# Moving a modulation slab from behind the linear half to behind the value products, in the prompt attention loop of a decoder step

## The chip, the cores and the metric

The kernel runs on one core of one Trainium2 chip. The metric is the device time of one execution in microseconds; a change is compared by the median of several runs. The engines are called as in the profile: PE is the matrix engine (TensorE), with PEld for its weight loads, DVE is VectorE, ACT is ScalarE, POOL is GpSimd, and SP is the engine whose queue issues most DMAs.

## The reference, cut to what matters

One step of a decoder layer for a prompt of 512 tokens and 32 sample tokens. The two groups share all weights. The parts that meet in the stage under study are these:

```python
mod = jax.nn.silu(c) @ w['w_ada'] + w['b_ada']            # six modulation vectors
sh1, sc1, g1, sh2, sc2, g2 = jnp.split(mod[:, None, :], 6, axis=-1)
...
y_a = (bg * v) @ w['w_out_conv']                           # the convolution branch's projection
...
s_s = jnp.einsum('bqgrd,bgqnkd->bgrqnk', q, k_sel) - slopes * s_dist
p_s = jax.nn.softmax(jnp.where(tok_valid, s_s, NEG), axis=(-2, -1))
o_s = jnp.einsum('bgrqnk,bgqnkd->bqgrd', p_s, v_sel)
s_w = jnp.einsum('bqgrd,bkgd->bgrqk', q, kw) - sl * w_dist
p_w = jax.nn.softmax(jnp.where(w_valid, s_w, NEG), axis=-1)
o_w = jnp.einsum('bgrqk,bkgd->bqgrd', p_w, vw)
o = gates[..., 0:1] * o_c + gates[..., 1:2] * o_s + gates[..., 2:3] * o_w
...
x = x + g1 * ((ga * y_a + gb * y_b) @ w['w_out'])
```

There are 16 heads in 4 groups of 4. Of the modulation vectors the later ones (for the gates and the second norm) are needed only after the attention, so their products with `w_ada` can be computed at any time before that.

## The kernel before, in words

The kernel is one long straight program. It is written line by line, and the framework that compiles it puts the instructions of each engine into an order of its own planning: it goes by the order in the program, and where an instruction would have to wait it may place a later one first. The order on the chip is then fixed.

The prompt attention is a loop (lines 1511 to 1531) over the 4 head groups `g` and, in each, the query blocks `i` = 3, 2, 1, 0 of 128 queries. One pair is a unit; block `i` attends to 128(i+1) keys, so block 3 is the largest. A unit is a generator in two halves (`unit`, line 1417):

- Scores. For each of the 4 heads and the 2 branches (selected and window) PE multiplies queries and keys into an accumulator `sp` (lines 1431 to 1439), DVE adds the distance penalty and takes the extremum (line 1444), and ACT takes the exponential with its sum (line 1445). Then DVE makes the factors `fac` (lines 1449 and 1450) and scales the eight probability tiles `P` (line 1457). Tiles of odd and of even blocks have eight buffers each.
- Value products. PE transposes the compressed branch's probabilities (`ctp`, line 1462), which ACT copies (`pct`), then for every 128 keys and each branch four transpositions into one accumulator (`ptp`, line 1472). Each such accumulator is copied to a tile `PT`, five times of six by ACT, the sixth time by DVE (`pev`, lines 1386 and 1388). Two products per 128 keys (`acc`, line 1466) and eight of the compressed branch (line 1482) gather the output; ACT and DVE move it to `oT` (lines 1484 and 1485).

Three further kinds of work are put between these in each iteration:

- A linear half (`oc_gen`, line 1366): 24 matmuls (lines 252 to 254) of the convolution branch's output projection, one half of the tokens for one block of 128 columns. Its weights come as 1 MB slabs, four in all, and are split by ACT and DVE into a high and a low part (lines 247 and 248). SP loads a tile `ga` for each half, and DVE multiplies by it (line 1378).
- A modulation slab (`mod_slab`, line 426): 32 matmuls (line 432) of `w_ada`, 256 columns a slab, run in four column strips of the array (128\*32); ACT copies the sum (`m`, line 434), and the slab before is finished by a transposition (`modq`, line 443) and two small DVE additions. SP loads a slab of 1 MB into one of three buffers `raw`, which the linear slabs use too.
- `presum` (line 561): copies of weights for later stages, a DMA by SP and an adding DMA by POOL.

The order in an iteration before the change is: scores of the unit, a linear half, a modulation slab, `presum`, the value products of the unit before. The accumulators of the linear half, `modp`, `modq`, `ctp`, `ptp` and some scores share five banks; two more serve scores, one serves `acc`.

Of the kernel before, what the change touches and what calls it, by code (L numbers as in the profile page):

```python
# [156 lines left out]
def build(tc, a, o):  # L157
# [19 lines left out]
    def tp_ps(nm):  # L177
        return ps.tile([128, 512], F32, tag="g", bufs=5, name=nm)
# [9 lines left out]
    def nm(s):  # L188
        uid[0] += 1
        return f"{s}_{uid[0]}"  # L190
# [44 lines left out]
    def slab(*key):  # L235
        nk, ncol = len(SLABS[key][1]), SLABS[key][2].shape[-1]
        v = raw_tile("raw")[:, 0:nk * ncol]
        last_slab[0] = queue(lambda: sync.dma_start(v, a["wt"][SLAB_AT[key], :, 0:nk * ncol]))
        return v.rearrange("p (k f) -> p k f", k=nk)
# [186 lines left out]
    def mod_slab(s, v=None):  # L426
        v = slab("ada", s) if v is None else v
        p = tp_ps(nm("modp"))
        for k in range(KC):
            for hh in range(2):  # L430
                j = (k % 2) * 2 + hh
                pe.matmul(p[32 * j:32 * j + 32, 0:128], lhsT=cT[:, k, :], rhs=v[:, k, hh * 128:(hh + 1) * 128], start=(k < 2), stop=(k >= 6))  # L432
        m4 = wpool.tile([128, 128], F32, tag="m4", bufs=2, name=nm("m4"))
        act.activation(m4, p[:, 0:128], AF.Copy)
        if modp:
            modp.pop()()
        modp.append(lambda: mod_fin(s, m4))
# [3 lines left out]
    def mod_fin(s, m4):  # L441
        q = tp_ps(nm("modq"))
        pe.transpose(q[:, 0:128], m4, ident)
        qv = q[:, 0:128].rearrange("p (a h n) -> p a h n", a=2, h=2)
        dst = modT[:, 2 * s:2 * s + 2, :]
        bb = badaT[:, 2 * s:2 * s + 2].rearrange("p (h x) -> p h x", x=1).broadcast_to([128, 2, 9])
        dve.tensor_add(dst, qv[:, 0, :, 0:9], bb)
        dve.tensor_add(dst, qv[:, 1, :, 0:9], dst)
# [112 lines left out]
    def presum(n=1):  # L561

        done = copied[:]
        del copied[:]
        for _ in range(min(n, len(pre_keys))):
            key = pre_keys.pop(0)
            w_ = len(SLABS[key][1]) // 4 * 128
            t = pre[key] = dr.tile([128, 1024], F32, name=nm("pre"))
            src = a["wt"][SLAB_AT[key], :, 0:4 * w_].rearrange("p (n f) -> p n f", n=4)
            dst = t[:, 0:2 * w_].rearrange("p (n f) -> p n f", n=2)  # L570
            with tc.issue_after(last_slab[0].ins):
                sync.dma_start(dst, src[:, 0:1].broadcast_to([128, 2, w_]))
            copied.append((dst, src[:, 1:4:2]))
        for dst, src in done:
            pool.dma_start(dst, src, accum_op=ALU.add)  # L575
# [762 lines left out]
    def k_stack(g):  # L1338
        gp, me = g // 2, slice((g % 2) * 64, (g % 2) * 64 + 64)
        kh, kl = ks_[g % 2]  # L1340
        for n, t in enumerate((kh, kl)):
            for b in range(2):
                sync.dma_start(t[b * 64:b * 64 + 64].rearrange("p b x -> p (b x)").bitcast(F32), k_dr[gp][n][me])
        return kh, kl

    def q_stack(g):
        gp, me = g // 2, slice((g % 2) * 64, (g % 2) * 64 + 64)
        t = qs_[g % 2]
        for n in range(2):
            sync.dma_start(t[n * 64:n * 64 + 64].rearrange("p r x -> p (r x)").bitcast(F32), q_dr[gp][n][me])  # L1350
        return t
# [38 lines left out]
    def cmp_probs(g, qs):  # L1390
        p = tp_ps(nm("cpt"))
        for r in range(4):
            pe.matmul(p[32 * r:32 * r + 32, :], lhsT=kcd[:, g, :], rhs=qs[:, r, :].bitcast(F32), start=True, stop=True)
        ct = at.tile([128, 512], F32, tag="PT", bufs=4, name=nm("cpT"))
        act.activation(ct, p, AF.Copy)
        cps = s_ps(nm("cps"))
        for i in range(4):
            pe.transpose(cps[:, i * 128:(i + 1) * 128], ct[:, i * 128:(i + 1) * 128], ident)
        pc = pcs[g % 2] if g else pc0
        v3 = pc.rearrange("p i r c -> p (i r) c")  # L1400
        m, sm = (at.tile([128, 16], F32, tag=n, bufs=2, name=nm(n)) for n in ("cm", "csm"))
        bc = lambda z: z.rearrange("p (n x) -> p n x", x=1).broadcast_to([128, 16, 32])
        cd = t_cd.rearrange("p i (x c) -> p i x c", x=1).broadcast_to([128, 4, 4, 32])
        sl = slr[:, g, :].rearrange("p (y r x) -> p y r x", y=1, x=1).broadcast_to([128, 4, 4, 32])
        dve.tensor_add(pc, cps.rearrange("p (i r c) -> p i r c", i=4, r=4), cd)
        dve.tensor_mul(pc, pc, sl)
        dve.tensor_reduce(m, v3, axis=AX.X, op=ALU.max)
        dve.tensor_sub(v3, v3, bc(m))
        act.activation(pc, pc, AF.Exp)
        dve.tensor_reduce(sm, v3, axis=AX.X, op=ALU.add)  # L1410
        dve.reciprocal(sm, sm)
        dve.tensor_mul(sm.rearrange("p (i r) -> p i r", i=4), sm.rearrange("p (i r) -> p i r", i=4), gtok[:, :, g * 12:(g + 1) * 12].rearrange("p i (r b) -> p i r b", b=3)[:, :, :, 0])
        dve.tensor_scalar_mul(sm[:, 0:4], sm[:, 0:4], rowv)
        pool.tensor_tensor(v3, v3, bc(sm), op=ALU.mult)
        return pc
# [95 lines left out]
    prev = None  # L1511
    nslab = 8
    ocf = oc_gen()
    for g in range(4):
        qs, ks = qst, kst
        pc = cmp_probs(g, qs) if g else first_pc
        for i in (3, 2, 1, 0):
            u = unit(g, i, ks, qs, pc) if g or i < 3 else first_unit
            if g or i < 3:
                next(u)  # L1520
            next(ocf, None)
            mod_slab(nslab, mods_ahead.pop(0) if mods_ahead else None)
            nslab += 1
            presum(g > 0 or i < 2)
            if prev is not None:
                next(prev, None)
            prev = u
            if g < 3 and i == 3:
                qst = q_stack(g + 1)
            if g < 3 and i == 2:  # L1530
                kst = k_stack(g + 1)
# [554 lines left out]
```

## Time and profile before

| what | us |
|---|---|
| median of 3 runs | 1193.41 (1191.88 to 1194.09) |
| the profiled execution | 1191.61 |
| its span in the profile | 1189.8 |
| the 512 slab matmuls of the loop (line 432), busy | 19.1 |
| the value products `acc` (line 1466) in the loop, busy | 44.4 |
| the transpositions `ptp` (line 1472) of tiles `P` in the loop, busy | 36.8 |

The times of the timeline are counted from the start of the span. A row of the timeline has the start, the duration, the engine, the line, the operation, the tiles written and read, the shape, the number of like instructions merged into the row, and in brackets the idle time ahead of it with what ended it. Matmuls are pipelined: the distance from one start to the next tells what one costs, and the duration, which overlaps the next one's, does not.

### The profile page before, as it was taken

The page shows a single profiled execution, that of the slowest core. Times are in us where ns is not written, and L with a number is a line of the kernel's source. Part 1 is how long each engine was busy: PE and PEld are TensorE (multiplying, and loading weights), DVE is VectorE, ACT ScalarE, POOL GpSimd, SP SyncE. Part 2 cuts the span into 40 slices and gives each one's busy share as a digit, 9 for nine tenths or more (in the row PEclk, how much of TensorE's full clock was granted, in tenths as well). Part 3 has the DMA queues.
Part 4 walks back from the last instruction along what each step waited for, and adds up shares of the span by engine and source line. Part 5 has one row for each costly group of instructions (what it writes and reads, how often), then busy time and mean ns, then how long its engine had stood idle before and what let it go on. Part 6 is the DMA issues. An engine that isn't in the chain of part 4 may idle for free.

```text
span 1189.8 us, 25820 instructions
## 1 busy us (share of the span) xinstructions
PE 1177.5 (99%) x10114; PEld 1094.1 (92%) x10114; DVE 854.2 (72%) x1927; ACT 641.0 (54%) x1302; POOL 103.8 (9%) x154
## 2 busy tenths in 40 slices
PE   9999999999999999999999999999999999999997
PEld 7999999999999888887777879999999999999996
DVE  2539986888775576686767866758848888887776
ACT  1416544665455333386766765527646566666541
POOL 1000151000000111020101100000010001001000
PEclk9999999999999999999999999999999999999999
DMA  9963465878656998979887779444356358349412
GB/s 334 368 230 125 143 221 161 256 239 245 212 193 192 357 371 315 304 216 263 223 221 224 209 201 315 172 163 169 91 150 200 129 141 242 119 126 219 173 54 75
DMA packets 86283, 248.81 MB, mean 209 GB/s; under 512 B 9480, under 2 KB 19592, under 8 KB 74522
## 3 DMA queue, kind: packets, MB, share of 16 engines
q1 hardware_dynamic: 73330, 222.77, 53.6%
q0 software_dynamic: 12112, 23.09, 12.1%
q8 instruction: 79, 1.29, 0.4%
q10 hardware_dynamic: 720, 1.31, 0.3%
q14 instruction: 42, 0.34, 0.1%
HBM read 216.33 MB, written 65.28 MB: 237 GB/s over the span
## 4 chain that ended last, share of the span: by engine, by line
PE 92%; DVE 4%; DMA 2%; ACT 1%; issue 1%; POOL 0%; DVEq 0%; ACTq 0%; POOLq 0%
PE wA L254 8%; PE wA L252 8%; PE wA L253 8%; PE phi L676 7%; PE lin L252 7%; PE lin L253 7%; PE lin L254 7%; PE wC L253 4%; PE wC L254 4%; PE wC L252 4%; PE acc L1466 3%; PE ptp L1472 3%; PE modp L432 2%; PE wB L252 2%; PE wB L254 2%; PE wB L253 2%
## 5 line engine op out<-in xcount | busy, mean ns | idle before, releaser
L412 ACT ACTIVATE Wh<-raw 128x1024 fp32r<-128x1024 f32 (+2 forms) x82 | 62.1, 757 | 49.7 <-PE wA L253 34.9
L413 DVE TENSOR_TENSOR Wl<-raw,Wh 128x1024 fp32r<-128x1024 f32 (+2 forms) x82 | 70.1, 855 | 21.9 <-ACT Wh L412 21.4
L301 ACT ACTIVATE work<-wA 128x272 f32<-128x272 f32 x102 | 40.1, 393 | 73.6 <-PE wA L254 73.4
L1445 ACT ACTIVATE P<-P,nms 128x384 f32<-128x384 f32 (+3 forms) x120 | 65.0, 545 | 20.1 <-DVE nms L1444 19.2
L1444 DVE CUSTOM_DVE_ANT_0 P<-sp,ta 128x384 f32<-128x384 f32 (+3 forms) x120 | 52.2, 469 | 30.2 <-PE sp L1432 22.7
L252 PE MATMUL lin<-h_h,wh 128*128 128x288 f32 (+1 forms) x240 | 71.5, 298 | 0.0
L413 DVE TENSOR_TENSOR wl<-ws,wh 128x1024 fp32r<-128x1024 f32 (+1 forms) x50 | 59.1, 1182 | 16.3 <-ACT wh L412 15.1
L412 ACT ACTIVATE wh<-ws 128x1024 fp32r<-128x1024 f32 (+1 forms) x50 | 51.3, 1026 | 33.8 <-PE wC L253 23.2
L253 PE MATMUL lin<-h_l,wh 128*128 128x288 f32 (+1 forms) x240 | 69.3, 289 | 0.0
L413 DVE TENSOR_TENSOR wl<-raw,wh 128x1024 fp32r<-128x1024 f32 (+2 forms) x56 | 65.9, 1177 | 4.5 <-ACT wh L412 4.2
L254 PE MATMUL lin<-h_h,wl 128*128 128x288 f32 (+1 forms) x240 | 69.1, 288 | 0.0
L247 ACT ACTIVATE wh<-raw 128x1024 fp32r<-128x1024 f32 (+1 forms) x43 | 41.9, 976 | 41.7 <-PE lin L253 25.8
L248 DVE TENSOR_TENSOR wl<-raw,wh 128x1024 fp32r<-128x1024 f32 (+1 forms) x43 | 48.3, 1123 | 21.0 <-ACT wh L247 20.8
L412 ACT ACTIVATE wh<-raw 128x1024 fp32r<-128x1024 f32 (+2 forms) x56 | 56.1, 1001 | 12.6 <-PE wB L253 5.1
L676 PE MATMUL phi<-gt,wphi 128*128 128x128 f32 x512 | 61.3, 277 | 0.0
L676 PEld LDWEIGHTS phi<-gt,wphi 128*128 128x128 f32 x512 | 59.1, 192 | 1.9 <-issue 1.1
L575 POOL DMA_DIRECT2D pre<-in_wt x28 | 27.4, 977 | 349.1 <-DMA pre<-in_wt 335.1
L252 PE MATMUL wA<-S_hi,Wh 128*128 128x272 f32 x184 | 53.3, 290 | 0.6 <-ACT work L301 0.6
L254 PE MATMUL wA<-S_hi,Wl 128*128 128x272 f32 x184 | 53.1, 289 | 0.0
L253 PE MATMUL wA<-S_lo,Wh 128*128 128x272 f32 x184 | 53.0, 289 | 0.0
L252 PEld LDWEIGHTS lin<-h_h,wh 128*128 128x128 f32 x240 | 45.6, 190 | 7.5 <-issue 6.2
L253 PEld LDWEIGHTS lin<-h_l,wh 128*128 128x128 f32 x240 | 45.2, 188 | 0.1
(586 smaller groups left out, 4366.0 us busy)
## 6 DMA issues: line engine op xcount, KB each, us to landing
raw<-in_wt SPq DMA_DIRECT2D x68, 1024.0 KB, 6.7
raw<-in_wt SPq DMA_DIRECT2D x24, 768.0 KB, 5.3
sraw<-in_cache_sel SPq DMA_DIRECT2D x64, 256.0 KB, 5.4
gt<-in_cache_cmp SPq DMA_DIRECT2D x60, 256.0 KB, 5.7
pre<-in_wt SPq DMA_DIRECT2D x20, 512.0 KB, 8.8
pre<-in_wt POOLq DMA_DIRECT2D x20, 512.0 KB, 7.0
wraw<-in_cache_winT SPq DMA_DIRECT2D x8, 1024.0 KB, 7.8
raw<-pre SPq DMA_DIRECT2D x20, 256.0 KB, 6.6
```

The lines of the kernel that those rows point to most:

```text
L247: act.activation(oh, view, AF.Copy)
L248: dve.tensor_sub(ol, view, oh.bitcast(F32))
L252: pe.matmul(p, lhsT=wh[:, k, :], rhs=xh, start=start, stop=False, **kw)
L253: pe.matmul(p, lhsT=wh[:, k, :], rhs=xl, start=False, stop=False, **kw)
L254: pe.matmul(p, lhsT=wl[:, k, :], rhs=xh, start=False, stop=stop, **kw)
L301: o_.snap_ops.append(act.activation(t, p, AF.Copy))
L412: act.activation(hi, src, AF.Copy)
L413: return dve.tensor_sub(lo, src, hi.bitcast(F32))
L676: pe.matmul(po[:, c0:c0 + 128], lhsT=w[:, ch], rhs=x[:, :, ch * 16:ch * 16 + 16], start=(n_ == 0 and ch == 0), stop=(n_ == 2 and ch == 7))
L1444: p_ops.append(dve.tensor_tensor_reduce(out=t[:, 0:n], in0=sps[br], in1=t_dist[:, 512 - n:512], scale=-hs, scalar=3e38, op0=ALU.add, op1=A ...
L1445: e_ops.append(act.activation(t[:, 0:n], t[:, 0:n], AF.Exp, scale=-1.0, bias=nms[:, c:c + 1], accum_out=sums[:, c:c + 1]))
L1466: pe.matmul(acc[br * 64:br * 64 + 64, :], lhsT=vtok[br][:, j, g * 64:(g + 1) * 64], rhs=pts_[br], start=(j == 0), stop=False)
```

## The change

The call of `mod_slab` and `presum` moves behind the step of the previous unit's value products. In the new order an iteration has: scores of the unit, a linear half, the value products of the unit before, a modulation slab, `presum`. In the first iteration there is no unit before, and nothing changes there.

```diff
             if g or i < 3:
                 next(u)
             next(ocf, None)
+            if prev is not None:
+                next(prev, None)
+            prev = u
             mod_slab(nslab, mods_ahead.pop(0) if mods_ahead else None)
             nslab += 1
             presum(g > 0 or i < 2)
-            if prev is not None:
-                next(prev, None)
-            prev = u
             if g < 3 and i == 3:
                 qst = q_stack(g + 1)
             if g < 3 and i == 2:
                 kst = k_stack(g + 1)
```

## The prediction

> **What bounds the kernel now.** I read the page first, then the busy time of each engine in the attention stage, then the idle waits of TensorE there, and last the order of the instructions around a few modulation slabs.
>
> ```profile
> span 1189.8 us, 25820 instructions
> PE 1177.5 (99%) x10114; PEld 1094.1 (92%) x10114; DVE 854.2 (72%) x1927; ACT 641.0 (54%) x1302; POOL 103.8 (9%) x154
> ```
> ```profile
> 515.00:718.00 203.00, 202.42 (x1755) 153.18 (x1753) 145.16 (x513) 139.55 (x385) 22.23 (x25) 1.00 0.80 225
> ```
> ```profile
> PE acc L1466 <- ACT PT L1386: 0.3, 1, 0.3
> PE sp L1431 <- DVE nms L1444: 0.3, 1, 0.3
> ```
>
> The second fence is the stage that the change touches, all sixteen units of it: its length, then the busy time of TensorE, of its weight loads, of VectorE, ScalarE and GpSimd, then the granted clock (1.00). TensorE is busy for 202.42 of 203.00 us, and the third fence holds the only two waits that its matmul row shows, 0.3 us each. A busy row is not yet a full engine, so I looked at the distances between starts in one iteration (group 1, query block 1):
>
> ```profile
> 593.45 0.30 PE L253 MATMUL lin<-yin_lo,wh 128*128 128x288 f32 x1
> 593.58 0.29 PE L254 MATMUL lin<-yin_hi,wl 128*128 128x288 f32 x1
> 593.80 1.08 PE L432 MATMUL modp<-raw,cT 128*32 128x128 f32 x32
> 594.82 0.33 PE L443 MATMUL modq<-ident,m 128*128 128x128 f32 x1
> 594.98 0.27 PE L1462 MATMUL ctp<-ident,pc 128*128 128x128 f32 x1
> 595.09 1.91 PE L1472 MATMUL ptp<-ident,P 128*128 128x128 f32 x16
> 596.93 1.57 PE L1466 MATMUL acc<-PT,vtok 128*64 128x512 f32 x4
> ...
> 649.18 1.08 PE L1466 MATMUL acc<-PT,vtok 128*64 128x512 f32 x4
> ```
>
> Here the order of before is seen: linear half, slab (modp, with the transposition modq of the slab before), then the value products of the unit before (ctp, ptp, acc). Linear matmuls follow each other every 0.13 us and everything else is as tight, with one exception: the first four value products took 1.57 us where the same four took 1.08 us one group later. So TensorE sets the end of this stage, nothing can be gained by hiding work behind it, and the change can gain or lose only what alters TensorE's own intervals: changes of array layout, and waits of the value products for their copies.
>
> **What the change does, part by part.** It adds and removes no instruction. The slab's 32 matmuls and the modq transposition go from ahead of the previous unit's value products to behind them, in 15 of 16 iterations (the first has no previous unit). From the start of modp to the start of ctp the block is 594.98 - 593.80 = 1.18 us. The value products start that much earlier, the next unit's scores start when they did. Priced step by step:
>
> (a) *Layout.* From the last linear matmul to modp it is 593.80 - 593.58 = 0.22 us instead of 0.13: 0.09 us for going from the full array (128\*128) to four column strips (128\*32). After the change a linear matmul is followed by ctp, full width.
>
> ```profile
> 641.34 0.39 PE L1431 MATMUL sp<-kh,qs 128*128 128x512 f32 x1
> 641.57 0.40 PE L1432 MATMUL sp<-kl,qs 128*128 128x512 f32 x1
> ```
> ```profile
> 580.04 0.40 PE L1431 MATMUL sp<-kh,qs 128*128 128x512 f32 x1
> 580.27 1.47 PE L1472 MATMUL ptp<-ident,P 128*128 128x128 f32 x12
> ```
>
> No row shows that pair; the nearest is a score matmul before a transposition, both of full width, and it takes 0.23 us like two scores in a row (641.57 - 641.34), so no extra. At the other end modp follows the two-strip products, where a full-width score follows now: a change of layout either way. The gain lies between 0 and 0.09 us an iteration; I take 0.09, from the nearest row. In 12 iterations (the other three are priced whole in b): -1.1 us.
>
> (b) *The three iterations of block 2 in groups 1 to 3.* Here the previous unit is the large one (block 3), and ScalarE is late:
>
> ```profile
> 576.75 0.28 PE L254 MATMUL lin<-yin_hi,wl 128*128 128x256 f32 x1
> 576.96 0.41 PE L432 MATMUL modp<-raw,cT 128*32 128x128 f32 x2
> 577.30 0.45 PE L1438 MATMUL sp<-kh,qs 128*128 128x384 f32 x1
> ...
> 577.85 1.07 PE L432 MATMUL modp<-raw,cT 128*32 128x128 f32 x30
> 578.85 0.33 PE L443 MATMUL modq<-ident,m 128*128 128x128 f32 x1
> ...
> 581.67 0.65 PE L1466 MATMUL acc<-PT,vtok 128*64 128x512 f32 x2
> ```
> ```profile
> 578.78 0.60 ACT L1445 ACTIVATE P<-P,nms 128x384 f32<-128x384 f32 x1
> ...
> 579.67 0.27 ACT L1463 ACTIVATE pct<-ctp 128x128 f32<-128x128 f32 x1
> 580.00 0.60 ACT L1386 ACTIVATE PT<-ptp 128x512 f32<-128x512 f32 x1
> 580.97 1.09 ACT L1386 ACTIVATE PT<-ptp 128x512 f32<-128x512 f32 x2 [0.37 <-PE ptp L1472]
> ```
>
> ScalarE runs the new unit's exponentials until 579.4, and only then the copies (pct, PT) that the value products read. Before, slab and scores covered that, and the first product started at 581.67. After, the transpositions can begin at 576.9; sixteen take 1.84 us (595.09 to 596.93), the scores placed among them some 1.3 us (the pair at 577.30 takes 0.55; three single ones follow, estimated at 0.25 each), so TensorE is ready at 580.1. The copies are not: pct can move up to some 579.5, two PT follow at 0.54 us (1.09 for two) by about 580.85. So the products start 0.82 us earlier, not 1.18: a loss of 0.36 us, three times, +1.1 us. The bounds are 0 (copies planned ahead of the exponentials) and 1.18 each.
>
> (c) *Group 1, block 1, the late product above.* Its second copy is VectorE's:
>
> ```profile
> 594.50 2.19 DVE L1457 TENSOR_SCALAR P<-P,fac 128x256 f32<-128x256 f32 x8
> ...
> 596.69 0.69 DVE L1388 COPY PT<-ptp 128x512 f32<-128x512 f32 x1
> ```
>
> The copy stands behind the eight scalings of the new unit and ends at 597.4. The scalings hang on that unit's scores, which don't move. TensorE would be ready at 593.71 + 0.11 + 1.84 = 595.7 and still get the copy at 597.4, and the slab comes on top afterwards: +1.2 us, once. Lower bound 0, if the copy is planned ahead.
>
> (d) *The four iterations of block 0.* ScalarE has a 1 us weight split at the front:
>
> ```profile
> 553.00 1.04 ACT L247 ACTIVATE wh<-raw 128x1024 fp32r<-128x1024 f32 x1
> ...
> 554.76 1.58 ACT L1386 ACTIVATE PT<-ptp 128x512 f32<-128x512 f32 x3 [0.15 <-PE ptp L1472]
> ```
> ```profile
> 555.97 1.08 PE L1466 MATMUL acc<-PT,vtok 128*64 128x512 f32 x4
> ```
>
> After the change the split still ends at 554.04; pct (0.28) and two copies put the products at about 555.5, against 555.97 now. They would start 0.47 us earlier instead of 1.18, a loss of 0.7 us unless the slab, which is next in the program and needs none of these copies, fills the hole. Four copies fit into the five shared accumulators with room for the slab once ctp is read, so I take 0 and keep 4 x 0.7 = 2.9 us as the other end. Block 3 has small value products (two copies) and the same filler: 0.
>
> (e) *Queues.* The slab's load (1 MB) waits on SP for a buffer that an earlier slab frees, and now frees later by one unit's value products, about 8.5 us for the largest (eight tiles, each four transpositions at 0.115 us and two products at 0.25, and small ends).
>
> ```profile
> 579.31 0.38 SPq L238 DMA_DIRECT2D raw<-in_wt  x1
> ...
> 594.41 0.33 SPq L1374 DMA_DIRECT2D ga<-ga_dr  x1
> ```
> ```profile
> raw<-in_wt SPq DMA_DIRECT2D x68, 1024.0 KB, 6.7
> ```
>
> The load at 579.31 goes out 0.5 us after a slab's last matmul (578.85, where modq follows it). It would go to some 588, land at 595 after 6.7 us, and still be ahead of the ga load queued behind it, which waits for its own tile until 594.41. With three buffers a slab is loaded two iterations ahead of its matmuls, over 20 us by the iterations above (modp at 576.96, 593.80 and then 12 us later), so a landing 8.5 us later is still early. SP's order and GpSimd's additions don't change. Price 0; without that slack it would be up to 6.7 us a load.
>
> **Sum.** -1.1 + 1.1 + 1.2 + 0 + 0 = +1.2 us on the profiled execution's 1191.61, which is 1192.8. That execution lies 1.8 us under the median shown (1193.41), so for a median I say **1194.6**.
>
> [...] One PT copy takes ScalarE 0.53 us (1.58 for three), the four transpositions and two products behind it take TensorE about 0.96 (0.46, from 1.84 for sixteen, and half of the 1.0 that four products take), so the copies do not set the pace unless they start late. [...]
>
> **The rivals.**
>
> *Slower: copies stay behind the new unit's work.* Place: the four block-0 iterations (d). If the slab isn't planned into the hole behind the weight split, 2.9 us come on top: 1197.5 (+0.34%). It decides from the point where more than half of them go unfilled. For it: TensorE takes its matmuls in order (the wait of 0.3 us for nms had linear work right behind it), and the plan missed the late copy in c already. Against it: score pieces are placed in such holes elsewhere (577.30).
>
> *Faster: the plan moves the copies ahead.* Then b and c cost nothing, the layout gains 15 x 0.09 = 1.35, and what is lost now goes: 0.49 in c (1.57 less 1.08), the two waits of 0.3, and the slab cut in two by scores in b, which takes 1.89 us from 576.96 to 578.85 of which the scores are 0.55, so 0.3 over an uncut 1.02, three times. -1.35 - 1.1 - 0.9 = -3.4 us: 1190.0.
>
> *It doesn't do what it says.* The order on an engine is planned when the kernel is compiled, not written line by line (the scores inside the slab show it). If the slab is taken as the filler of the value products' first wait, it runs nearly where it did: 1193.4.
>
> *TensorE has room after all.* Its weight loads are busy 153.18 of 203.00 us, 75%, beside 99.7% for its matmuls. If that quarter were free, the slab could vanish from the path between products and scores: 15 x 1.18 = 17.7 us, 1175.7. [...] The starts 0.13 and 0.23 us apart without gaps speak against it here: long matmuls simply need few loads.
>
> **How the numbers follow.** A measurement of this kernel can tell about 0.2%, 2.4 us, from no change. Forecast with the third rival, both within that: 0.55. Slower by the first rival, or by several of b to d at their upper ends: 0.25. Faster by the second: 0.18, by the fourth: 0.02. So faster 0.20, same 0.55, slower 0.25. The range takes in the first two rivals and a little of the spread of the runs (1191.88 to 1194.09): 1189.5 to 1198.2.
>
> **What would show it.** Right: linear to ctp at 0.13 us; products at 580.85 or so in the block-2 iterations; a stretch of the same stage between 202 and 207 us; PE waits for PT growing from 0.3 to about 3 us. Wrong: copies standing ahead of exponentials and scalings (then faster), waits for PT in the block-0 iterations too (slower), or a difference that lies outside the stage.

## The result, and the profile after

The changed kernel takes **1203.87 us** (median of 6 runs, 1202.09 to 1207.71), the kernel before 1192.74 us in the runs beside it (6 runs, 1191.33 to 1194.09). The ratio is 1.0092, with a 95% interval of 1.008 to 1.0104: the change costs 11 us. The forecast was 1194.6, in a range of 1189.5 to 1198.2. Beside the runs further down, the kernel before had medians of 1192.74 to 1193.97; every ratio is to the kernel before in the same rounds, and a difference between medians of different rounds is good to about 1 us.

The head of the page after, then two views of the attention stage: its row with busy times (up to the point where the kernel before stood at 718.25, which is 728.58 here), and the waits of TensorE in it (total, times, longest; `nms` is the extremum that a scoring on VectorE writes):

```profile
span 1200.3 us, 25830 instructions
PE 1180.9 (98%) x10114; PEld 1095.2 (91%) x10114; DVE 856.4 (71%) x1927; ACT 639.0 (53%) x1302; POOL 103.8 (9%) x154
```
```profile
515.00:728.00 213.00, 206.81 (x1758) 155.11 (x1758) 147.74 (x514) 138.37 (x387) 22.25 (x25) 1.00 0.77 210
```
```profile
PE acc L1466 <- ACT PT L1386: 3.7, 4, 1.9
PE lin L252 <- DVE nms L1444: 1.8, 2, 1.1
PE ptp L1472 <- ACT pct L1463: 0.7, 1, 0.7
```

The span grew by 10.5 us, the stage by as much (728.58 less 718.25 is 10.3), and the rest of the kernel is unchanged. In the stage TensorE now stands idle for 6.2 us (213.00 less 206.81; 0.6 before), and its busy time grew by 4.4 although its matmuls are the same ones: a busy row that grows without new work is a row with stretched intervals.

To see where the time went I cut the stage at the last linear matmul of each iteration, so that every piece holds one linear half, one slab, one unit's value products and about one unit's scores. For instance, in group 1 the piece with the value products of block 3 took 593.58 - 576.75 = 16.83 us before (rows of the prediction), and after:

```profile
581.37 0.28 PE L254 MATMUL lin<-yin_hi,wl 128*128 128x256 f32 x1
...
597.63 0.30 PE L254 MATMUL lin<-yin_hi,wl 128*128 128x288 f32 x1
```

That is 16.26 us. (The end is the start of the last linear matmul in both.) Pieces are named by the block whose value products they hold. The piece of block 0 lies in the block-3 iteration, that of block 3 in the block-2 iteration, and so on. Blocks 0 and 3 follow each other, and scores slip between them, so they are added. Sums over the groups, in us (of blocks 1 and 0 the last group has no linear half of this loop behind it and is missing):

| kernel | blocks 0 and 3 | block 2 | block 1 |
|---|---|---|---|
| before | 91.86 | 47.14 | 43.10 |
| after | 96.31 (+4.45) | 51.32 (+4.18) | 44.49 (+1.39) |

Two places of about equal size, then, each with its own mechanism in the trace.

**Place one: a weight split that waits for its load, ahead of the copies.** Group 2, value products of block 2, ScalarE and TensorE after:

```profile
652.30 0.49 ACT L1445 ACTIVATE P<-P,nms 128x256 f32<-128x256 f32 x1
...
654.93 1.06 ACT L247 ACTIVATE wh<-raw 128x1024 fp32r<-128x1024 f32 x1 [2.04 <-DMA raw<-in_wt]
655.90 0.26 ACT L1463 ACTIVATE pct<-ctp 128x128 f32<-128x128 f32 x1
656.05 2.05 ACT L1386 ACTIVATE PT<-ptp 128x512 f32<-128x512 f32 x4
```
```profile
652.68 0.30 PE L254 MATMUL lin<-yin_hi,wl 128*128 128x288 f32 x1
652.82 0.27 PE L1462 MATMUL ctp<-ident,pc 128*128 128x128 f32 x1
652.92 1.91 PE L1472 MATMUL ptp<-ident,P 128*128 128x128 f32 x16
656.70 1.56 PE L1466 MATMUL acc<-PT,vtok 128*64 128x512 f32 x4 [1.86 <-ACT PT L1386]
...
677.58 0.30 PE L252 MATMUL lin<-yin_hi,wh 128*128 128x288 f32 x1
```

The split (wh, line 247) waits 2.04 us for its slab to land and then works 1.06 us. The copies pct and PT stand behind it, though the transpositions they read began at 652.8, and TensorE stands still for 1.86 us. The split is the first of a new slab. The linear half that ends at 652.68 and the one from 663.22 on still read weights of the slab before, split at 610.88; the half that reads the new ones starts at 677.58, over 22 us later: nobody was in a hurry for the split. It merely stood first in the queue: in these rows ScalarE begins none of the copies in the 2.04 us in which the split waits, and takes them behind it (655.90 and 656.05).

The load is late because the block-2 slab, whose buffer it takes, is now later. Its issue on SP (SPq is SP's queue), before (632.21) and after (647.67), and the same split before. Counted from the last linear matmul of the iteration (629.66 and 637.99), the load goes out after 2.55 us before and after 9.68 us now, 7.1 us later:

```profile
632.21 1.04 SPq L238 DMA_DIRECT2D raw<-in_wt  x1
```
```profile
647.67 0.33 SPq L238 DMA_DIRECT2D raw<-in_wt  x1
```
```profile
640.49 1.06 ACT L247 ACTIVATE wh<-raw 128x1024 fp32r<-128x1024 f32 x1 [0.53 <-DMA raw<-in_wt]
```

Already before, the split waited 0.53 us for this load, behind all copies of block 3's value products. The load had no slack at all at its first reader in this group, and that row stood in the trace when I predicted.

**Place two: the scores of block 2 start late.** The start of group 1's block-3 iteration, TensorE and then VectorE, before:

```profile
568.71 1.04 PE L1472 MATMUL ptp<-ident,P 128*128 128x128 f32 x8
569.50 0.71 PE L1438 MATMUL sp<-kh,qs 128*128 128x384 f32 x2
570.05 0.52 PE L1439 MATMUL sp<-kl,qs 128*128 128x384 f32 x2
...
571.22 1.30 PE L1466 MATMUL acc<-PT,vtok 128*64 128x512 f32 x4
```
```profile
570.43 0.56 DVE L1444 CUSTOM_DVE_ANT_0 P<-sp,ta 128x384 f32<-128x384 f32 x1 [0.64 <-PE sp L1439]
...
572.01 3.26 DVE L1457 TENSOR_SCALAR P<-P,fac 128x512 f32<-128x512 f32 x8
```

and after:

```profile
569.43 1.03 PE L1472 MATMUL ptp<-ident,P 128*128 128x128 f32 x8
570.22 0.42 PE L1438 MATMUL sp<-kh,qs 128*128 128x384 f32 x1
570.57 0.62 PE L432 MATMUL modp<-raw,cT 128*32 128x128 f32 x10
571.12 1.07 PE L1466 MATMUL acc<-PT,vtok 128*64 128x512 f32 x2
572.12 0.86 PE L432 MATMUL modp<-raw,cT 128*32 128x128 f32 x22
...
574.79 0.62 PE L1439 MATMUL sp<-kl,qs 128*128 128x384 f32 x2
...
577.87 0.39 PE L252 MATMUL lin<-yin_hi,wh 128*128 128x256 f32 x1 [1.08 <-DVE nms L1444]
```
```profile
573.41 3.26 DVE L1457 TENSOR_SCALAR P<-P,fac 128x512 f32<-128x512 f32 x8
...
577.27 0.54 DVE L1444 CUSTOM_DVE_ANT_0 P<-sp,ta 128x384 f32<-128x384 f32 x1
```

Before, eight score matmuls filled the hole between the transpositions and products of block 0, and VectorE did three scorings (line 1444, 570.43 to 572.01) ahead of the 3.26 us of scalings for the large block 3. After, the slab fills that hole, cut in two, with a change of array layout at each cut (128\*32 to 128\*64 at 571.12, and back at 572.12). The first complete score pair comes at 574.79, VectorE has begun the scalings at 573.41, and its first scoring stands behind them at 577.27. The linear half, which shares accumulators with the scores, waits 1.08 us for that scoring. The piece as a whole grew by 2.64 us (569.18 to 581.37, against 567.20 to 576.75). The wait is less than half of that; one more pair of scores lies in the piece, some 0.35 us (575.24 to 575.59), and most of the rest are the stretched intervals of slab and products from 570.57 to 574.79, where each cuts the other: 4.22 us with 0.36 of a score in them, against 1.18 (567.42 to 568.60) and 1.67 (571.22 to 572.89) before.

### The profile page after: what moved, and what is told of

It reads as the page before. It is cut to its first block, busy times and chain, and to the rows that moved or that the text cites. A ratio compares the mean times of both kernels' runs of the same rounds, so it can differ in the third digit from the quotient of the medians.

```text
span 1200.3 us, 25830 instructions
## 1 busy us (share of the span) xinstructions
PE 1180.9 (98%) x10114; PEld 1095.2 (91%) x10114; DVE 856.4 (71%) x1927; ACT 639.0 (53%) x1302; POOL 103.8 (9%) x154
## 4 chain that ended last, share of the span: by engine, by line
PE 87%; DVE 5%; DMA 4%; ACT 2%; issue 1%; SPq 0%; ACTq 0%; DVEq 0%; POOL 0%
PE wA L254 8%; PE wA L252 8%; PE wA L253 8%; PE lin L252 6%; PE phi L676 6%; PE lin L253 6%; PE lin L254 6%; PE wC L253 4%; PE wC L254 4%; PE wC L252 4%; PE acc L1466 3%; PE ptp L1472 2%; PE modp L432 2%; PE wB L252 2%; PE wB L254 2%; PE wB L253 2%
## 5 line engine op out<-in xcount | busy, mean ns | idle before, releaser
L1466 PE MATMUL acc<-PT,vtok 128*64 128x512 f32 x160 | 50.8, 612 | 3.7 <-ACT PT L1386 3.7
```

The source lines that it names most:

```text
L1466: pe.matmul(acc[br * 64:br * 64 + 64, :], lhsT=vtok[br][:, j, g * 64:(g + 1) * 64], rhs=pts_[br], start=(j == 0), stop=False)
```

## The experiments

Each edit is told against the kernel before or the changed one. Theory 1 is place one (the load, through ScalarE's queue), theory 3 is place two. Theory 2 is the prediction's own: copies that stand behind exponentials and scalings once the slab ahead of them is gone.

**The split alone put right (split_tied).** The changed kernel, with the first split of each linear slab placed behind the last value-product copy on ScalarE:

```diff
+    pev_act = [None]
...
-            act.activation(out, in_, AF.Copy)
+            pev_act[0] = act.activation(out, in_, AF.Copy)
...
-                wh, wl = split(so[:, :, kk * 128:(kk + 1) * 128])
+                with tc.issue_after(pev_act[0].ins) if pev_act[0] and kk == 0 else ExitStack(): wh, wl = split(so[:, :, kk * 128:(kk + 1) * 128])
```

> The changed kernel with one thing more: the first weight split of each linear slab (line 247) is queued on ScalarE behind the last value-product copy before it in the program, instead of in the middle of, or ahead of, the copies of block 2. TensorE's order stays. Theory 1 (a late load: the slab's buffer comes free later, the linear slab that takes it is loaded later, its split waits for the load at the head of ScalarE's queue, and the copies behind it wait too): the value products of block 2 go back from 8.1 and 8.7 us to 6.3 in groups 0 and 2; in group 1 they stay near 8 since VectorE's copy is late by itself. About 4 us less than the changed kernel, 1199.5. Theory 2 (the value products simply lost their cover, copies wait for exponentials and scalings): no more than 1 us less, 1203. Theory 3 (the loss lies in the scores of block 2, which come after the slab): no change, 1204.

Measured: 1198.09 us (1197.5 to 1199.41), ratio to before 1.0034 [1.0023, 1.0046]: 5.8 us less than the changed kernel. ScalarE in group 2 and TensorE's waits in the stage:

```profile
650.16 0.28 ACT L1463 ACTIVATE pct<-ctp 128x128 f32<-128x128 f32 x1 [0.23 <-PE ctp L1462]
650.65 2.06 ACT L1386 ACTIVATE PT<-ptp 128x512 f32<-128x512 f32 x4 [0.22 <-PE ptp L1472]
```
```profile
PE lin L252 <- DVE nms L1444: 1.8, 2, 1.0
PE ptp L1472 <- ACT pct L1463: 0.7, 1, 0.7
PE acc L1466 <- ACT PT L1386: 0.2, 1, 0.2
```

The copies follow their transpositions, and the waits for PT fell from 3.7 to 0.2 us. Block 2's pieces go from 51.32 to 46.52, below the 47.14 of before. Blocks 0 and 3 stay at 97.12. Place one is shown, and it is somewhat over half of the loss (5.8 us by the medians, 6.5 when each kernel is held against the kernel before of its own rounds).

**One block moved at a time (only_i3, only_i2, only_i1).** The kernel before, with the new order in one block's iterations only; for block 3:

```diff
+            if i == 3 and prev is not None: next(prev, None)
             mod_slab(nslab, mods_ahead.pop(0) if mods_ahead else None)
             nslab += 1
             presum(g > 0 or i < 2)
-            if prev is not None:
-                next(prev, None)
+            if i != 3 and prev is not None: next(prev, None)
```

> The kernel before, with the slab moved behind the value products in the block-3 iterations alone (groups 1 to 3; in group 0 there are no value products yet). Theory 3 (there the slab takes the place of the scores of block 2 that were placed between the transpositions and products of block 0; VectorE then gets those scores only behind eight scalings of 3.3 us, and TensorE waits with linear work queued behind): 1 to 2 us a group, 1195 to 1198, with a wait of a linear matmul for the score op of about 1 us in two groups. Theories 1 and 2: within 1 us of the kernel before, 1193.

> The kernel before, with the slab moved behind the value products of block 3 in the block-2 iterations alone (all four groups). Theory 1: this slab is the one whose buffer the next linear slab takes, so its load goes out some 8 to 13 us later than before, and the split waits in ScalarE's queue ahead of the copies of block 2: 2 us each in groups 0 to 2, 1196 to 1199, with value products of block 2 at 8 us in place of 6.3 to 6.8. Theory 2: 0.4 us a group as forecast, 1194. Theory 3: no change, 1193.

> The kernel before, with the slab moved behind the value products of block 2 in the block-1 iterations alone. Theory 1: its buffer goes to a modulation slab that is not needed for two iterations, so nothing waits for the load: 1193 (within 1 us). Theory 2: the copies of block 2 lose their cover: 1.2 us in group 1 (VectorE's copy) and up to 1.2 in the others, 1194 to 1197. Theory 3: no change, 1193.

Measured: block 3 alone 1202.01 us (4 runs; the other two have 10), ratio 1.006 [1.0039, 1.0081]; block 2 alone 1196.62, 1.0014 [1.0004, 1.0024]; block 1 alone 1194.32, 1.0003 [0.9993, 1.0013]. Block 1's time lies at the lower end of what theory 2 said (1194 to 1197) and can't refute it, but the trace does for its place: block 2's pieces, where the copies would have lost their cover, take 46.25 against 47.14 before, and in group 1 12.21 against 12.23. Block 2's time came out as theory 1 said, but not in its place. The splits do wait for their loads (1.95 us ahead of 594.34, 1.57 ahead of 647.67), yet block 2's pieces are 47.28, as before: in this kernel the block-1 iterations still have the slab ahead of the products, and TensorE works on it meanwhile. Its stage lost 1.4 us in all, with block 1's pieces 1.8 us longer (44.87 against 43.10); the other 2.7 us by which the profiled execution is longer lie behind the stage. By these runs the late split costs block 2's products only where the slab ahead of them is gone as well. Block 3 cost twice what theory 3 said, and its trace shows why: here too splits stand ahead of other work and wait for their loads.

```profile
589.55 1.06 ACT L247 ACTIVATE wh<-raw 128x1024 fp32r<-128x1024 f32 x1 [2.10 <-DMA raw<-in_wt]
...
645.48 1.06 ACT L247 ACTIVATE wh<-raw 128x1024 fp32r<-128x1024 f32 x1 [2.24 <-DMA raw<-in_wt]
```

So this run mixes both mechanisms, and the next four kernels separate them by means of the tie (the split placed behind the copies, as in split_tied). `before_tied` is the kernel before with the tie, the others add the new order in the blocks named.

> The slab comes late in the four block-3 iterations alone, as in the run before it that gave 1202.0, and the first weight split of each linear slab is queued on ScalarE behind the last value-product copy of the unit. Theory 3 (the scores of block 2 come later there, and TensorE then waits for VectorE's read of them) sees only the waits for the split gone: it had three such iterations 1.3 to 1.9 us longer up to the end of the linear half, 4.4 in all, so 1193.5 + 4.4 = some 1198, with TensorE still waiting 1 to 2 us for VectorE's nms. Theory 1 alone (a late load at the head of ScalarE's queue is all of it) gives 1193.5.

> The order of before, with the first weight split of each linear slab queued behind the last value-product copy. Theory 1: the wait of a split for its load is only 0.5 us in one unit of the kernel before, and behind cover there, so no change, 1193.0 to 1193.5. If the tie itself is worth something (or costs something), it shows here: more than 2.5 us either way, and the run with the tie in the changed kernel has to be read against it.

> The slab comes late in the iterations of blocks 2, 1 and 0, as in the change, and not in those of block 3; the split is tied behind the copies. Theory 3: the change with the tie stood at 4.6 us over the kernel before, 4.4 of them from block 3, so this comes to within 1 us of before: 1192.5 to 1194.5. A rival, by which the copies that come late in blocks 2 to 0 (b to d of the prediction) are the rest: 1196 to 1198.

> The slab comes late in the iterations of blocks 1 and 0 alone, with the tie. There the change of layout from full array to strips stays away (0.09 us, eight times) and one late copy of VectorE stays: 1192.5 to 1194. Theory 2 (copies behind scalings and splits cost in blocks 1 and 0) gives 1195 to 1196.

| kernel | us (10 runs each) | ratio to before | blocks 0 and 3 | block 2 | block 1 |
|---|---|---|---|---|---|
| before_tied | 1193.76 | 1.0002 [0.9991, 1.0013] | 93.58 | 47.49 | 42.05 |
| i3_tied | 1195.45 | 1.0009 [0.9999, 1.0019] | 95.57 | 47.48 | 42.04 |
| no_i3_tied | 1192.08 | 0.998 [0.9969, 0.9992] | 91.81 | 46.22 | 44.09 |
| i01_tied | 1193.8 | 0.9994 [0.9983, 1.0006] | 92.29 | 46.52 | 43.84 |

The tie by itself changes nothing in the total. With it, block 3 alone falls from 1202.01 to 1195.45, so 6.6 us of that run came with the waiting splits. Part of these is the clock: in the profiled execution of only_i3 it fell after one of the waits (last section). It was 0.66 in the mean from 594 to 599, which makes an estimated loss of 1.7 us; in i3_tied it was 1.00 from 590 to 600. What is left, 1.7 us over before_tied, lies between the two expectations (0 and 4.4). In the full change block 3 costs more: 1198.09 (split_tied) against 1192.08 (no_i3_tied), 6 us. By the pieces it is 5.3 us against 2.0. The pieces of block 0 are as long in both (34.09 in i3_tied, 34.21 in split_tied), but they start from different lengths: 30.02 in before_tied, 28.63 in no_i3_tied. That is 1.5 us of the difference. The rest comes in the following pieces of block 3: 61.48 in i3_tied against 63.56 in before_tied, so 2.1 us are given back there, and 62.91 (split_tied) against 63.18 (no_i3_tied) in the full order, where next to nothing is. In i3_tied these products still have a slab ahead of them and run without a break; group 1:

```profile
579.25 1.08 PE L432 MATMUL modp<-raw,cT 128*32 128x128 f32 x32
...
588.93 0.50 PE L1431 MATMUL sp<-kh,qs 128*128 128x512 f32 x1
```

Slab and products take 588.93 - 579.25 = 9.68 us there. In the changed kernel they take 592.58 - 581.49 = 11.09, with the copies behind the exponentials:

```profile
581.49 0.27 PE L1462 MATMUL ctp<-ident,pc 128*128 128x128 f32 x1
...
592.49 0.33 PE L443 MATMUL modq<-ident,m 128*128 128x128 f32 x1
592.58 0.48 PE L1431 MATMUL sp<-kh,qs 128*128 128x512 f32 x1
```

That the slab ahead is what makes this part of the difference is read from these rows; no run tested it alone.

**Is it the order of slab and scores, or the cover? (behind_scores_tied)** In the changed kernel with the tie, the slab of the block-3 iterations goes still further back, behind the next unit's scores:

```diff
             if g or i < 3:
                 next(u)
+            if i == 2 and prev is not None and g:
+                mod_slab(nslab, mods_ahead.pop(0) if mods_ahead else None)
+                nslab += 1
+                presum(1)
             next(ocf, None)
...
+            if i < 3 or g == 0:
+                mod_slab(nslab, mods_ahead.pop(0) if mods_ahead else None)
+                nslab += 1
+                presum(g > 0 or i < 2)
```

> The change with the split tied, but in the three block-3 iterations that have a unit before them the slab goes one step further back: behind the next unit's scores, ahead of its linear half. The small value products of block 0 lose the slab ahead of them exactly as in the change, but the scores follow them at once. Theory 3 (the slab pieces stand where the scores of block 2 stood, and VectorE starts on them later): the 6 us between the change with the tie and the same without block 3 come back, 1192 to 1194. The rival (the value products of block 0 need the slab ahead of them as cover): they stay lost, 1197 to 1199.

Measured: 1193.21 us (1192.33 to 1194.38), ratio 0.9988 [0.9977, 1.0]. VectorE's scorings of block 2 are ahead of the scalings again:

```profile
569.14 0.56 DVE L1444 CUSTOM_DVE_ANT_0 P<-sp,ta 128x384 f32<-128x384 f32 x1
...
571.20 3.26 DVE L1457 TENSOR_SCALAR P<-P,fac 128x512 f32<-128x512 f32 x8
```

Here all 15 slabs stand behind the value products, and nothing is lost. Blocks 0 and 3 take 92.69, against 97.12 in split_tied and 91.81 in no_i3_tied: the products of block 0 needed the slab as cover for 0.9 us at most, and the other 4.4 hang on the slab standing where the scores of block 2 stood. Place two is shown as well. The run puts two things right at once, though, the late scores and the slab that is cut among the products; it doesn't tell how much each of them cost.

**The split without block 3 (no_i3), and which block pays (i2_tied).** no_i3 is no_i3_tied without the tie, and i2_tied moves block 2 alone, with it.

> The slab comes late in the iterations of blocks 2, 1 and 0, not in block 3, and the split is not tied. Theory 1: the load is still freed late by the block-2 slab, so the split waits at the head of ScalarE's queue as in the change: 1195 to 1198, with waits of TensorE for PT of 2 to 4 us. If the late load only hurts together with the late scores: 1192 to 1193.

> The slab comes late in the iterations of block 2 alone, with the tie. From the earlier runs: blocks 2, 1 and 0 together gave 1192.1 and blocks 1 and 0 together 1193.8, so if they add, block 2 alone gives some 1192.3. If block 2's move pays only through the other two, 1193.5 to 1194.

Measured: no_i3 1195.65 us, ratio 1.0013 [1.0004, 1.0023]; i2_tied 1193.85, 0.9997 [0.9987, 1.0006]. Taking the tie away costs 3.6 us also without the late scores, and block 2's pieces account for it: 49.73 against 46.22. There the wait can be short and the price still large, since the split itself stands ahead of the last copy:

```profile
648.04 2.07 ACT L1386 ACTIVATE PT<-ptp 128x512 f32<-128x512 f32 x4 [0.22 <-PE ptp L1472]
650.81 1.06 ACT L247 ACTIVATE wh<-raw 128x1024 fp32r<-128x1024 f32 x1 [0.70 <-DMA raw<-in_wt]
651.78 0.58 ACT L1386 ACTIVATE PT<-ptp 128x512 f32<-128x512 f32 x1
```

i2_tied is 2.8 us below only_i2, so the tie takes away what block 2 cost alone (block 1's pieces go from 44.87 to 42.04). It missed the 1192.3 that adding up would give and lies in the other range that I named, 1193.5 to 1194: the parts do not add to the last microsecond.

**The best order once more (no_i3_tied_again).**

> The same kernel as in no_i3_tied, in more rounds. If the gain of 0.2% there is real: a ratio of 0.997 to 0.999. If it came from the spread of runs (its two halves, i01_tied and i2_tied, gave 0.9994 and 0.9997): 0.9985 to 1.0005.

Measured: 1192.35 us (1190.67 to 1193.83, 12 runs), ratio 0.9987 [0.9976, 0.9999]. The ratio lies in both of the expected ranges, so this run does not decide between them. Moving the slab in blocks 2, 1 and 0 and tying the split stood below the kernel before both times, by 1.9 and 1.2 us with intervals that end just under 1: at the edge of what can be told. Against the changed kernel it is over 11 us.

## Why the prediction was wrong

The forecast of +1.2 us met +11. Taken by its own steps:

- **(e) Queues, priced 0: the step that failed first.** I wrote that a landing 8.5 us later "is still early", because a slab is loaded two iterations ahead of its matmuls. I had measured the slack at the matmuls. The load's first reader is the split on ScalarE, and there the slack was already gone (0.53 us of waiting at 640.49 before). The upper end that I named, up to 6.7 us a load, was not carried into the range. Measured: 5.8 us in all (split_tied), 3.6 without block 3. The delay of the load was well estimated (8.5 us said, 7.1 measured in group 2); what was wrong is that it would be free.
- **(d) "Block 3 has small value products and the same filler: 0": the second failure.** I asked only whether the products had cover, and they did. I did not ask what filled the hole before: the scores of block 2, which VectorE needed ahead of its scalings. A slab in their place delays VectorE, not TensorE, at first: in group 1 the first scoring went from 570.43 to 577.27, and TensorE's wait of 1.08 us came behind that (577.87). Measured: 6 us in the full change (split_tied less no_i3_tied; less behind_scores_tied it is 4.9). The products that (d) prices itself are those of block 1, in the block-0 iterations: there the slab did fill the hole, as I took it, but by cutting through the products. In group 1 of the changed kernel:

```profile
610.80 0.27 PE L1462 MATMUL ctp<-ident,pc 128*128 128x128 f32 x1
...
613.75 0.41 PE L432 MATMUL modp<-raw,cT 128*32 128x128 f32 x2
...
617.65 1.06 PE L1393 MATMUL cpt<-qs,kcd 128*32 128x512 f32 x8
```

  Slab and products take 617.65 - 610.80 = 6.85 us where before they took 5.58 (606.02 to 611.60): +1.27 in this one iteration, which is in the pieces of block 1 (+1.39). The pieces of block 1 in groups 0 and 2 change by -0.15 and +0.36. (The other end of (d), 4 x 0.7, is 2.8 and not 2.9; it plays no part.)
- **(a) Layout: right, and larger.** Linear matmul to ctp takes 0.14 us (652.68 to 652.82), as said. I missed that modq is now followed by scores after 0.09 us (592.49 to 592.58), where ctp followed it after 0.16 before (594.82 to 594.98). In an undisturbed iteration, block 2 of group 2, the piece is 11.59 us before and 11.39 with the tie: 0.2 us, not 0.09.
- **(b) Block 2's iterations, +0.36 us three times: about right.** In group 1, slab and products take 11.09 after; before, 589.19 - 576.96 = 12.23 less 1.42 of scores among them (the pair of 0.55, 0.31 for one, 0.56 for two), so 10.81: +0.28. By the same count it is -0.2 in group 2 and +0.7 in group 3, +0.8 in all against +1.1. The copies do stand behind the exponentials, but the first product starts 2.22 us behind the last linear matmul in group 1 (583.59 less 581.37), not the 4.1 that 580.85 stood for, since the scores that I had placed among the transpositions are not there.
- **(c) Group 1, VectorE's late copy, +1.2 us: a third of it.** From the linear half's last matmul the piece is 13.04 us after, 12.47 with the tie, 12.23 before; with the 0.2 us of layout that is some 0.4 for the copy, and the rest of the loss there was the split.
- **The signs I had named.** PE's waits for PT "growing from 0.3 to about 3 us" came, 3.7, and would have counted as confirmation. They were a split's waits and not the exponentials' or scalings': the tie alone takes them to 0.2. The stage at 213 us, beyond 202 to 207, was the sign that spoke true.
- **The rivals.** *Slower* had the right side and the wrong place: the block-0 iterations gave 1.4 us of the 11 (pieces of block 1). *It doesn't do what it says* is refuted where products follow the linear half at once (652.68 to 652.82); in the block-3 iterations something like it happened, ten of the slab's matmuls ahead of the first product (570.57), and that is place two. *TensorE has room* is refuted: it said 1175.7, and the change cost 11 us. That the quarter of the stage without weight loads is free time was its assumption, and no run shows it; in the stage before, about every matmul has its load (1753 to 1755), of 188 ns for a linear matmul and 135 ns for a value product, and these start 0.13 and 0.25 us apart without gaps. *Faster* said 1190.0; the best order found gives about half of that gain, with the split tied and block 3 left as before (1192.1 and 1192.4). That the copies, at 0.53 us each, do not set the pace unless they start late is borne out: behind_scores_tied moves all 15 slabs behind the value products and stands at 0.9988.

What stays open: why 2 us of block 3's cost come back in the next iteration when only block 3 is moved. The rows above suggest the slab's cover; no run isolates it. Open too is how place two divides between the late scores and the cut slab.

## What to carry to other kernels

When a block of work moves, follow every transfer whose buffer it frees to the transfer's first reader, and read that reader's wait: here ScalarE left the copies behind a late load waiting for 2.04 us, over 22 us before a matmul needed the data. Whether that costs anything depends on the work that the bounding engine has meanwhile: with the slab ahead (only_i2) block 2's products lost next to nothing by it (47.28 us against 47.14). Ask also what stood in the place that the moved block will take, and which other engine had been fed from there. A predicted total of waits isn't a confirmation of its cause: put the cause right by itself, as the tie does here, and look whether the waits go.

## Of the hardware, not expected

In only_i3, TensorE stood idle for 2.06 us, and then the clock fell. Its rows, and the row of the stretch 595 to 598 (the granted clock is the third number from the end):

```profile
591.16 0.30 PE L252 MATMUL lin<-yin_hi,wh 128*128 128x288 f32 x1
593.52 0.48 PE L1431 MATMUL sp<-kh,qs 128*128 128x512 f32 x1 [2.06 <-DVE nms L1444]
...
595.63 0.44 PE L253 MATMUL lin<-yin_lo,wh 128*128 128x288 f32 x1
595.87 0.44 PE L254 MATMUL lin<-yin_hi,wl 128*128 128x288 f32 x1
```
```profile
595.00:598.00 3.00, 3.00 (x20) 2.70 (x22) 0.98 (x7) 1.96 (x8) 0.00 (x0) 0.50 0.00 0
```

Linear matmuls start 0.24 us apart in place of 0.13, at a clock of 0.50, after TensorE has already been at work again for over a microsecond. In the changed kernel no fall followed a wait of 1.86 us (656.70): the clock was 1.00 from 656 to 660. One wait of 2.06 us with a fall behind it and one of 1.86 us without are too few to name a bound, and no run shows that the wait is what made the clock fall.
